# Attention with its exponentials split between ScalarE and VectorE: the planner's costs set anew, DMAs planned by a clock, five buffers for VectorE's weights

## The chip, the cores and the metric

The kernel runs on one core of one Trainium2 chip. The metric is the device time of one execution in microseconds (us), lower is better.

## The reference

Multi-query attention: 8 batches, 1024 positions, 16 heads of 64, all heads of a batch share one key and one value matrix.

```python
q = q.transpose(0, 2, 1, 3)                       # (8, 16, 1024, 64)
scores = np.matmul(q, k.transpose(0, 1, 3, 2)) / np.sqrt(head_dim)
weights = np.exp(scores - np.max(scores, axis=-1, keepdims=True))
weights = weights / np.sum(weights, axis=-1, keepdims=True)
attn_out = np.matmul(weights, v)
```

## The kernel before, in words

**Work.** Two heads make a pair: 64 pairs, 8 of each batch. A pair has 8 key tiles of 128 positions, and each key tile two halves of 512 queries. The unit of work is a score tile, 128 keys by 2 heads by 512 queries in fp32: 64 x 8 x 2 = 1024 of them. TensorE makes one with two matmuls of 64 rows (`score`, L554 to L563) in one of three PSUM slots. Then its exponential is taken, in one of two ways. ScalarE does it in one instruction (`exp_act`, L577) and writes fp16 weights to one of 20 `wt` buffers (`ABUFS`). VectorE does it in groups of two key tiles, four score tiles, called duos in the code: four instructions turn scores into the bits of a first approximation (`fixed`, L586, the planner's "z"), and a polynomial over the mantissas corrects it (`poly`, L599 to L623): f, m, their product (L615), and two halves of l (L617). A linear term is done by GpSimd in four pieces (`linear`, L630). The correction is added to the weights by an accumulating DMA, one for each half (`add`, L642); in the first group and those of the last two pairs VectorE adds it itself (L621). The weights lie in `wd` buffers (`DBUFS`, 4).

**Value products.** `value` (L647) multiplies the weights by the values, which carry a column of ones, so that the row sums come out too. 16 blocks of 128 queries make a pair; 7 blocks (`NG`) share an accumulator, and there are two accumulators. When a group of blocks is complete, VectorE takes reciprocals (L675) and normalises into `osb` (L685), and SP writes a finished pair to memory (L702). `osb` holds three pairs.

**Inputs.** Queries come in groups of 4 pairs: GpSimd loads four parts of a group, converting to fp16 (`load_part`, L488, four buffers), and SP turns each part by a DMA transpose into `qt` (`trans_q`, L497, three buffers). Keys of the next batch are loaded, copied and turned likewise (L429, L443, L451).

**Order.** Every engine's program order is written by a planner that runs before the kernel is built. `plan` (L70) simulates TensorE, ScalarE, VectorE and GpSimd with costs given as constants at the head of the file: `ACT_P` is the spacing of exponentials, `ACT_L` the time from a start to the free slot, `QK_P` a score, `AV_B` one block of a value product, `SWITCH` a change between the two, `PE_L` from a score's start to its reader's, `STEPS` and `VEC` VectorE's instructions. At each step TensorE takes a score for ScalarE, a score for VectorE or a value product; `LAG` is how many pairs the products stay behind the exponentials, `LEAD` how far VectorE's groups may run ahead of ScalarE's pair. A score for VectorE is planned when VectorE is due (`Z_PE`) and ScalarE has work ahead (`Z_ACT`). Additions, loads and transposes aren't part of this simulation: `with_dmas` (L331) puts them into the finished list, additions as soon as GpSimd has room, transposes when the exponentials have come so far as `transfers` (L317) says, in pairs. The list is then issued in order (L727), and each engine and queue executes its part in that order, with semaphores for the data. Within this list the planner's own times play no part any more.

Of the kernel before, what the change touches and what calls it, by code (L numbers as in the profile page):

```python
# [10 lines left out]
FP16 = mybir.dt.float16  # L11
# [6 lines left out]
P = 128  # L18
# [6 lines left out]
VEC = dict(z=1.13, rec=0.12, norm=0.55)  # L25
STEPS = (1.13, 1.13, 1.13, 2.2, 1.13, 1.13, 1.13, 1.13)
VEC_L = 0.19
VEC_DEP = 0.12
ADD_L = 12.0
POOL_S, POOL_F, POOL_L, POOL_D = 0.15, 1.05, 0.12, 1.0  # L30
# [3 lines left out]
ABUFS, DBUFS = 20, 4  # L34
LAG, END = 1.0, 6.0
LEAD, LEAD_0, LEAD_END = 2.5, 1.5, 10.0
FIRST_Q = 6.0
# [3 lines left out]
REM = (4, 3, 2, 2)  # L41
Z_GAP, Z_PE, Z_ACT = 2, 2.0, 1.3
ACC_L = 0.25
FAR = 1e9
# [24 lines left out]

def plan(NP, NKT, stats=None):  # L70
# [13 lines left out]

    pe = act = 0.0
# [11 lines left out]
    gap = 99  # L97
# [12 lines left out]
    pool = lock = 0.0  # L110
# [3 lines left out]
    while todo_g or groups:  # L114
        if pe <= dve:
            T = pe
            prog = ap + (na / nap if ap >= 0 else 0)
            if not vunits and not over:
                lead = min(LEAD if prog > 4 else LEAD_0, LEAD * (NP - prog) / LEAD_END) if duos else 0
                pd = max(dlast + 1, math.ceil(ap + lead))  # L120
                okay = pd < NP and (len(duos) < DBUFS or all(used[t] == NB for t in duos[-DBUFS]))
                if pd // 4 == 0:
                    okay = okay and T >= FIRST_Q * pd
                else:
                    okay = okay and prog >= 4 * (pd // 4) - QLEAD and T >= FIRST_Q * min(pd, 6)
                if pd <= ap:
                    okay = okay and pd == ap and len(ajs) >= 2 and ap < NP - 1
                if okay and prog < NP - STOP:
                    js = [ajs.pop(-2), ajs.pop(-1)] if pd == ap else [NKT - 2, NKT - 1]
                    if pd == ap:  # L130
                        nap -= 4
                    d = len(duos)
                    duos.append([pd * NKT + j for j in js])
                    mine[pd] = mine.get(pd, []) + js
                    for n, j in enumerate(js):
                        owner[pd * NKT + j] = d
                    vunits = [(d, i) for i in range(4)]
                    dlast = pd
# [14 lines left out]
            free = [s for s in range(3) if slot[s] <= T + (SWITCH if mode != "qk" else 0)]  # L153
            kind = None
            if (free and vunits and gap >= Z_GAP and not zs and dve <= T + PE_L + Z_PE and act > T + Z_ACT
                    and len(steps) <= REM[vunits[0][1]]):
                kind = "z"
            elif free and units:
                kind = "act"
            elif free and vunits and ap == NP - 1 and not ajs and not zs and len(steps) <= REM[vunits[0][1]]:  # L160
                kind = "z"
# [9 lines left out]
            for grp in groups:  # L171
# [16 lines left out]
            av = tav <= T + (SWITCH if mode != "av" else 0) and (  # L188
                nv < NB * NKT * (prog - lag) or over
            )  # L190
            do = None
            if kind and (
                mode == "qk" or len(free) >= 2 or not av
                or act - T - SWITCH - PE_L < AV_B * 6 + MARGIN
            ):
                do = "qk"
            elif mode == "qk" and units and min(slot) - T < WAIT:
                pass
            elif av:
                do = "av"  # L200
                first = min(slot)
                if units and first - T < AV_B * 6 and (
                    act - max(first, T) - SWITCH - PE_L < AV_B * 3 + MARGIN
                ):
                    do = None
            if do == "qk":
                s = min(free, key=lambda s: slot[s])
                st = max(T + (SWITCH if mode != "qk" else 0), slot[s])
                pe, mode = st + QK_P, "qk"
                if kind == "z":  # L210
                    d, i = vunits.pop(0)
                    slot[s] = FAR
                    zs.append((st + PE_L, s, (d, i)))
                    gap = 0
                    emit(st, "qk", duos[d][i // 2], i % 2, s)
                else:
                    u = units.pop(0)
                    na += 1
                    act = max(act, st + PE_L)
                    emit(act, "act", *u)  # L220
                    slot[s] = ready[u] = act + ACT_L
                    act += ACT_P
                    gap += 1
                    emit(st, "qk", *u, s)
            elif do == "av":
                st = max(T + (SWITCH if mode != "av" else 0), tav)
# [4 lines left out]
                pe = st + AV_B * nb + (AV_1 if mode == "qk" else 0)  # L231
# [5 lines left out]
                if not left:  # L237
                    acc[a] = FAR
                    r = pe - AV_B + PE_L
# [5 lines left out]
        else:  # L245
            T = dve
            z = [x for x in zs if x[0] <= T]
# [36 lines left out]
            elif what == "step":  # L284
# [8 lines left out]
                if n in (0, 1):  # L293
                    ready[duos[x[0]][n]] = dve + VEC_L + ADD_L * (not late)
# [5 lines left out]
            else:  # L300
                nxt = [x[0] for x in zs + evs if x[0] > T] + [pe + 1e-6] * (pe > T)
                nxt += [x for x in (*avail.values(), pool) if T < x < FAR]
                dve = max(min(nxt, default=0.0), T + 1e-3)
                last = None
        if max(pe, dve) > 900:
            raise RuntimeError((pe, dve, ap, len(duos), steps, halves, vunits, groups, slot))
    for _, k, segs, a, kind in evs:
# [5 lines left out]
    units = [2 * (NKT - len(mine.get(p, []))) for p in range(NP)]  # L313
    return with_dmas(ops, duos, units, direct, NP, NKT), duos


def transfers(NP):  # L317
    QP, HP = 4, 8
    res = []
    for g in range(1, NP // QP):  # L320
        for i in range(QP):
            at = QP * (g - 2) + i + 0.2 if g > 1 else 0.15 + 0.5 * i
            res += [(at, "loadq", g, i), (at + 0.75, "turnq", g, i)]
    for b in range(1, NP // HP):
        at = HP * (b - 1)
        res += [(at + 1.5, "loadk", b), (at + 2.2, "copyk", b), (at + 2.5, "turnk", b, 0),
                (at + 3.5, "turnk", b, 1), (at + 2.9, "loadv", b)]
    return sorted(res)


def with_dmas(ops, duos, units, direct, NP, NKT):  # L331
    fs = [t for t, _, op in ops if op[0] == "l"] + [FAR]
    todo = transfers(NP)
    cost = dict(loadq=0.85, loadk=0.85, copyk=0.95, loadv=1.2)
    res, adds, loads, turns, gone = [], [], [], [], set()
    n, pool, done = 0, 0.0, {}
    last = ops[-1][0]
    for t, _, op in ops + [(last + 20.0 * i, 0, ("end",)) for i in range(1, 4)]:
        if op[0] != "end":
            res.append(op)  # L340
        if op[0] == "l":
            n += 1
            pool = max(pool, t + POOL_S) + POOL_F
        if op[0] == "step" and op[2] in (4, 5) and op[1] not in direct:
            adds.append((t + STEPS[op[2]], op[1], op[2] - 4))
        if op[0] == "act":
            p = op[1] // NKT
            done[p] = done.get(p, 0) + 1
            prog = p + done[p] / units[p]
            while todo and todo[0][0] <= prog:  # L350
                x = todo.pop(0)
                (turns if x[1][:4] == "turn" else loads).append(x[1:])
        while True:
            at = max(pool, t)
            room = fs[n] - at if n < len(fs) else FAR
            if adds and adds[0][0] <= t + 0.3 and room > POOL_D:
                _, d, h = adds.pop(0)
                res.append(("add", d, h))
                pool = at + POOL_D
            elif not adds and loads and room > cost[loads[0][0]] + 0.1:  # L360
                x = loads.pop(0)
                res.append(x)
                gone.add(x)
                pool = at + cost[x[0]]
            else:
                break
        for x in list(turns):
            if ("load" if x[0] == "turnq" else "copy") + x[0][4:] in {y[0] for y in gone if y[1:] == x[1:len(y)]}:
                res.append(x)
                turns.remove(x)  # L370
    assert not (adds or loads or turns or todo), (adds, loads, turns, todo)
    return res
# [3 lines left out]
def kernel(  # L376
# [43 lines left out]
    behind: dict = {}  # L420
    acc: dict = {}
    rec: dict = {}
    left = [NB] * NP

# [20 lines left out]
    def trans_k(b, x):  # L445
# [48 lines left out]
    def trans_q(g, i):  # L494
        if g and i == 0:
            place_q(g)
        nc.sync.dma_start_transpose(  # L497
            out=of_pair(qt[g], i), in_=qn[g, i].rearrange("p c x -> p (c x)")
        )

# [9 lines left out]
    def load_first():  # L510
# [12 lines left out]
        st["k16"] = consts.tile([P, NKT, 2, D], FP16, name="k160")  # L523
# [53 lines left out]
    def exp_act(t, c):  # L577
        nc.scalar.activation(  # L578
            out=wt[t][:, :, c * QC : (c + 1) * QC], in_=sc.pop((t, c)), func=EXP, scale=ascale
        )  # L580
# [59 lines left out]
    def add(d, h):  # L640
        x = slice(h * 2 * S, (h + 1) * 2 * S)
        nc.gpsimd.dma_start(  # L642
            out=flat(wd[d].bitcast(I16))[:, x], in_=tmp[d, "l"].bitcast(I16)[:, x],
            accum_op=ALU.add,
        )
# [58 lines left out]
    ops, duos = plan(NP, NKT)  # L704
    groups = grouped(NP)
# [91 lines left out]
```

## Time and profile before

| | us |
|---|---|
| median of 3 runs (lowest, highest) | 771.21 (769.87, 773.09) |
| the profiled execution | 771.49 |
| its span, first to last instruction | 769.6 |
| ScalarE busy | 751.5 |
| VectorE busy | 713.8 |
| TensorE busy (matmul) | 677.7 |
| GpSimd busy | 380.0 |

The profile is of one execution. "Busy" is the union of an engine's instructions; matmuls are pipelined, so TensorE's figure is not that of a full array. L578 is line 578 of the kernel before. A row of the groups gives line, engine, operation, output<-input, shapes and count, then busy time, the mean of one in ns, and the idle time of the engine just before such instructions with what ended it. A wait row gives who waited, for whom, then the total in us, how often, and the longest. A timeline row gives the start, the time to the end of the merged instructions, engine, line, operation and count, and in brackets the idle time before.

### The profile page before, as it was taken

Reading aid. Unit: us, or ns where it says so; the run is one execution under the profiler, and the core shown is the slowest. Engines: PE = TensorE matmul, PEld = TensorE weight load, DVE = VectorE, ACT = ScalarE, POOL = GpSimd, SP = SyncE. Lnnn points to the kernel's source line nnn. Section 1 sums busy time; section 2 is a strip of 40 time slices with the busy share of each in tenths; the row PEclk is TensorE's granted clock in tenths of the full one; section 3 lists DMA queues with packets and bytes.
Section 4 is the critical chain, followed back from the end, with each engine's and each line's share of the span. In section 5 each row is a group of like instructions: output and inputs, shape, how many; then the busy total and the mean of one; then the engine's idle time right before and its main releaser. Section 6 shows DMA issues by size and latency. Waiting matters only on the chain.

```text
span 769.6 us, 23528 instructions
## 1 busy us (share of the span) xinstructions
PE 677.7 (88%) x10256; PEld 414.3 (54%) x10256; DVE 713.8 (93%) x797; ACT 751.5 (98%) x819; POOL 380.0 (49%) x393
## 2 busy tenths in 40 slices
PE   6869989889989999989999899899898899989987
PEld 2435555555555555555555555555555555555555
DVE  5969999998999999998998999999999999999997
ACT  7969999999999999999999999999999999999996
POOL 3144545655447545556446546465454555453400
PEclk9979999999999999999999999999999999999999
DMA  9878899999999999999898999999989999866443
GB/s 168 120 133 155 150 186 163 169 175 174 162 162 170 191 180 152 193 145 203 144 180 150 190 185 156 170 188 169 182 144 175 186 178 167 163 131 134 112 102 93
DMA packets 185046, 124.07 MB, mean 161 GB/s; under 512 B 89328, under 2 KB 172400, under 8 KB 184944
## 3 DMA queue, kind: packets, MB, share of 16 engines
q0 software_dynamic: 42880, 69.87, 56.7%
q1 hardware_dynamic: 140480, 51.92, 35.5%
q8 instruction: 80, 1.31, 0.7%
q10 hardware_dynamic: 1584, 0.79, 0.4%
q14 instruction: 22, 0.18, 0.1%
HBM read 37.75 MB, written 33.55 MB: 93 GB/s over the span
## 4 chain that ended last, share of the span: by engine, by line
ACT 76%; issue 12%; PE 6%; DMA 1%; DVE 0%; SPq 0%; ACTq 0%
ACT wt L578 76%; PE sc L558 3%; PE acc L666 3%; DMA qt<-qn 1%; DVE osb L685 0%; SPq L702 0%; DVE rec L675 0%; ACTq L578 0%; SPq L497 0%
## 5 line engine op out<-in xcount | busy, mean ns | idle before, releaser
L578 ACT ACTIVATE wt<-sc 128x1024 f16<-128x1024 f32 x816 | 749.0, 1266 | 8.3 <-PE sc L558 8.3
L558 PE MATMUL sc<-qt,k2t 64*128 64x512 f16 x2048 | 372.0, 385 | 82.1 <-ACT wt L578 57.8
L630 POOL TENSOR_SCALAR l<-f 128x1024 f16<-128x1024 uint16 x196 | 212.4, 1083 | 293.0 <-DVE m L615 134.2
L666 PE MATMUL acc<-v,wt 128*128 128x65 f16 x6528 | 307.7, 195 | 0.9 <-issue 0.7
L666 PEld LDWEIGHTS <-wt 128*128 128x128 f16 x6528 | 236.8, 98 | 129.0 <-issue 128.5
L586 DVE TENSOR_SCALAR wd<-sc 128x1024 uint16<-128x1024 f32 x208 | 253.6, 1219 | 31.3 <-PE sc L558 30.3
L558 PEld LDWEIGHTS <-k2t 64*128 64x128 f16 x2048 | 129.1, 93 | 183.4 <-issue 136.6
L617 DVE TENSOR_TENSOR l<-m,l 128x2048 int16<-128x2048 f16 x104 | 126.0, 1213 | 7.6 <-POOL l L630 7.1
L615 DVE TENSOR_TENSOR m<-f,m 128x4096 f16<-128x4096 uint16 x52 | 118.7, 2283 | 0.2
L642 POOL DMA_DIRECT2D wd<-l x98 | 94.5, 964 | 39.2 <-DVE l L617 24.9
L666 PE MATMUL acc<-v,wd 128*128 128x65 f16 x1664 | 100.1, 194 | 0.0
L685 DVE TENSOR_TENSOR osb<-acc,rec 128x448 f32<-128x448 f32 (+4 forms) x165 | 91.6, 566 | 2.6
L666 PEld LDWEIGHTS <-wd 128*128 128x128 f16 x1664 | 69.4, 97 | 32.8 <-issue 32.8
L488 POOL DMA_DIRECT2D qn<-in_q_dram x60 | 59.9, 1000 | 18.7 <-DMA qt<-qn 9.5
L604 DVE TENSOR_SCALAR f<-wd 128x4096 uint16<-128x4096 uint16 x52 | 64.0, 1231 | 0.3
L607 DVE TENSOR_SCALAR m<-f 128x4096 f16<-128x4096 uint16 x52 | 64.0, 1230 | 0.3
L675 DVE RECIPROCAL rec<-acc 128x7 f32<-128x7 f32 (+1 forms) x147 | 28.4, 195 | 3.7 <-PE acc L666 3.5
L437 POOL DMA_DIRECT2D v<-in_v_dram x8 | 9.3, 1163 | 0.0
L621 DVE TENSOR_TENSOR wd<-wd,l 128x2048 uint16<-128x2048 uint16 x6 | 7.2, 1210 | 0.0
L429 POOL DMA_DIRECT2D k<-in_k_dram x7 | 5.7, 821 | 0.1
L544 PE MATMUL kps<-ident,k 128*128 128x128 f16 x8 | 1.2, 308 | 4.1 <-DVE k L532 4.1
L443 POOL COPY k<-k 128x64 f16<-128x64 f16 x7 | 4.2, 599 | 1.2 <-DMA k<-in_k_dram 1.0
(19 smaller groups left out, 17.8 us busy)
## 6 DMA issues: line engine op xcount, KB each, us to landing
wd<-l POOLq DMA_DIRECT2D x98, 512.0 KB, 6.6
out_dram<-osb SPq DMA_DIRECT2D x63, 512.0 KB, 6.4
qn<-in_q_dram POOLq DMA_DIRECT2D x63, 256.0 KB, 7.3
v<-in_v_dram POOLq DMA_DIRECT2D x8, 128.0 KB, 6.6
qt<-qn SPq DMA_TRANSPOSE x63, 5.2
k<-in_k_dram POOLq DMA_DIRECT2D x7, 128.0 KB, 8.7
osb<-in_q_dram ACTq DMA_DIRECT2D x2, 256.0 KB, 4.0
osb<-in_k_dram SPq DMA_DIRECT2D x2, 128.0 KB, 3.1
```

Source lines behind the costliest of these rows:

```text
L488: nc.gpsimd.dma_start(out=qn[g, i], in_=q[b, :, 2 * QP * r : 2 * QP * (r + 1), :].rearrange("(c p) h d -> p c (h d)", p=P)[:, n * i : n * ...
L558: nc.tensor.matmul(sc[t, c][:, h, :].rearrange("p (i x) -> p i x", x=P), keys(p // HP, h, j), queries(p, c)[64 * h : 64 * h + 64, :, :], s ...
L578: nc.scalar.activation(out=wt[t][:, :, c * QC : (c + 1) * QC], in_=sc.pop((t, c)), func=EXP, scale=ascale)
L586: behind["dve"] = nc.vector.tensor_scalar(out=wt[t].bitcast(U16)[:, :, c * QC : (c + 1) * QC], in0=sc.pop((t, c)), scalar1=vscale, scalar2 ...
L604: i = V.tensor_scalar(out=new(d, "f", U16, 1), in0=z, scalar1=1023, scalar2=None, op0=ALU.bitwise_and)
L607: i = V.tensor_scalar(out=new(d, "m", FP16, 1), in0=tmp[d, "f"], scalar1=-ONE, scalar2=1.0 / ONE, op0=ALU.add, op1=ALU.mult)
L615: i = V.tensor_tensor(out=tmp[d, "m"], in0=tmp[d, "f"], in1=tmp[d, "m"], op=ALU.mult)
L617: i = V.tensor_tensor(out=tmp[d, "l"].bitcast(I16)[:, h], in0=tmp[d, "m"][:, h], in1=tmp[d, "l"][:, h], op=ALU.mult)
L630: n = nc.gpsimd.tensor_scalar(out=tmp[d, "l"][:, x], in0=tmp[d, "f"][:, x], scalar1=GB / ONE, scalar2=GA, op0=ALU.mult, op1=ALU.add,)
L642: nc.gpsimd.dma_start(out=flat(wd[d].bitcast(I16))[:, x], in_=tmp[d, "l"].bitcast(I16)[:, x], accum_op=ALU.add,)
L666: nc.tensor.matmul(acc[k][:, n + x - lo, 0 : D + 1], w[:, h, i * P : (i + 1) * P], kst[p // HP]["v"][:, j, 0 : D + 1], start=first and x = ...
L685: behind["dve"] = nc.vector.tensor_tensor(out=osb[:, x % (OSB * NB) : x % (OSB * NB) + m, :], in0=a[:, n : n + m, 0:D], in1=r[:, n : n + m ...
```

## The change

The constants are replaced: spacing of exponentials 0.915 to 0.905, the latencies split by who reads, `DBUFS` 4 to 5, `LAG` 1.0 to 1.7, and others. The planner's choice at TensorE compares when ScalarE would run dry for either order, and a slot that becomes free while TensorE waits costs a `WAKE`. `with_dmas` is gone: additions, loads and transposes are issued inside the simulation by `issue`, with a clock for SP (`sp`), for the DMA engines busy with additions (`busy`) and for those busy with a transpose (`hold`). In the kernel a transpose gets two dependencies more, on the last addition issued and on an exponential two back in the list, and an addition that was held back by a transpose gets one on such an exponential. The first batch's doubled keys (`k160`) lie in the part of `osb` that pair 2 uses later.

By the order of instructions that comes out, the changed kernel has 54 groups on VectorE (52 before), 216 score tiles there (208), 808 exponentials on ScalarE (816), and 102 accumulating DMAs (98). The value products, loads and transposes are the same in number.

```diff
-ACT_P, ACT_L = 0.915, 1.15
-QK_P, AV_B, AV_1, SWITCH, PE_L = 0.23, 0.035, 0.02, 0.10, 0.51
-MARGIN, WAIT = 0.35, 0.3
+ACT_P, ACT_L, ACT_R = 0.905, 1.07, 1.15
+QK_P, AV_B, SWITCH, PE_L, PE_Z, PE_R = 0.215, 0.03, 0.11, 0.49, 0.44, 0.24
+MARGIN, WAIT, WAKE = 0.3, 0.5, 0.27
...
-ADD_L = 12.0
+POOL_D = dict(add=1.0, loadq=0.85, loadk=0.85, copyk=0.95, loadv=1.2)
+ADD_0, ADD_1, ADD_L = 2.7, 2.2, 6.0
+TURN_0, TURN_1, TURN_L, LOAD_L = 1.0, 4.0, 8.0, 8.0
...
-ABUFS, DBUFS = 20, 4
-LAG, END = 1.0, 6.0
-LEAD, LEAD_0, LEAD_END = 2.5, 1.5, 10.0
-FIRST_Q = 6.0
+ABUFS, DBUFS = 20, 5
+LAG, END = 1.7, 8.0
+LEAD, LEAD_0, LEAD_END = 3.0, 1.5, 10.0
+FIRST_Q, FIRST_G = 3.5, 22.0
...
-Z_GAP, Z_PE, Z_ACT = 2, 2.0, 1.3
-ACC_L = 0.25
+Z_GAP, Z_PE, Z_ACT = 2, 2.0, 1.0
+ACC_L = 0.15
...
-            at = QP * (g - 2) + i + 0.2 if g > 1 else 0.15 + 0.5 * i
-            res += [(at, "loadq", g, i), (at + 0.75, "turnq", g, i)]
+            at = QP * (g - 2) + 0.85 * i - 0.6 if g > 2 else 1.2 + 0.7 * i if g > 1 else 0.02 + 0.01 * i
+            res += [(at, "loadq", g, i), (at + (0.7 if g > 1 else 0.0), "turnq", g, i)]
...
+    def issue(t):
+        nonlocal pool, sp, busy, hold
+        while todo_d and todo_d[0][0] <= prog:
+            x = todo_d.pop(0)[1:]
+            (turns if x[0][:4] == "turn" else loads).append(x)
+        if turns and t >= max(sp, busy - TURN_0):
+            x = turns[0]
+            at = landed.get(x[1:3] if x[0] == "turnq" else ("copyk", x[1]), FAR)
+            if at <= t:
+                turns.pop(0)
+                emit(t, *x)
+                if x[0] == "turnq":
+                    freed.append(t + TURN_L)
+                sp = t + TURN_0
+                hold = t + TURN_1
+        if pool > t or halves and zs:
+            return
+        if adds and adds[0][0] <= t and t >= hold - ADD_0:
+            at, d, h = adds.pop(0)
+            emit(t, "add", d, h, at < hold - ADD_0)
+            pool = t + POOL_D["add"]
+            busy = max(busy, t + ADD_0) + ADD_1
+            ready[duos[d][h]] = busy + ADD_L
+        elif loads and not adds and can(loads[0], t):
...
-            if kind and (
-                mode == "qk" or len(free) >= 2 or not av
-                or act - T - SWITCH - PE_L < AV_B * 6 + MARGIN
-            ):
+            if kind == "z":
                 do = "qk"
-            elif mode == "qk" and units and min(slot) - T < WAIT:
-                pass
+            elif kind == "act":
+                s = min(range(3), key=lambda s: slot[s])
+                at = aq if slot[s] <= aq else slot[s] + WAKE
+                if av:
+                    then = after if slot[s] <= after else slot[s] + WAKE
+                if slot[s] <= aq:
+                    do = "qk" if mode == "qk" or len(free) >= 2 or not av or then + PE_L > act - MARGIN else "av"
+                elif av and (then <= at + 0.02 or then + PE_L <= act):
+                    do = "av"
+                elif slot[s] - T < WAIT:
+                    do = "qk"
             elif av:
                 do = "av"
...
-def with_dmas(ops, duos, units, direct, NP, NKT):
...
+    def after(i, xs):
+        for x in xs:
+            tc.add_manual_dep(
+                i.ins, x.ins.name,
+                mybir.DependencyInfo(mybir.DependencyClass.Sync, mybir.DependencyReason.DATA),
+                reason="transposes and additions apart",
+            )
...
-        nc.sync.dma_start_transpose(
+        i = nc.sync.dma_start_transpose(
             out=of_pair(qt[g], i), in_=qn[g, i].rearrange("p c x -> p (c x)")
         )
+        after(i, past[-2:-1] + added[-1:])
...
-        st["k16"] = consts.tile([P, NKT, 2, D], FP16, name="k160")
+        st["k16"] = osb[:, 2 * NB : 2 * NB + NKT, :].bitcast(FP16).rearrange("p c (r d) -> p c r d", r=2)
...
-    def add(d, h):
+    def add(d, h, held):
         x = slice(h * 2 * S, (h + 1) * 2 * S)
-        nc.gpsimd.dma_start(
+        added.append(nc.gpsimd.dma_start(
             out=flat(wd[d].bitcast(I16))[:, x], in_=tmp[d, "l"].bitcast(I16)[:, x],
             accum_op=ALU.add,
-        )
+        ))
+        if held:
+            after(added[-1], past[-2:-1])
```

More of the change, by code (lines that the diff above doesn't have):

```diff
@@ L109, in plan @@
     direct: set = set()
-    pool = lock = 0.0
+    pool = lock = sp = busy = hold = prog = 0.0
+    todo_d = transfers(NP)
+    freed = [0.0] * 4
+    adds: list = []
+    loads: list = []
+    turns: list = []
+    landed: dict = {}
     dlast = -1
@@ L225, in plan @@
             elif do == "av":
-                st = max(T + (SWITCH if mode != "av" else 0), tav)
+                st = aa
                 grp, n, j = pick
@@ L293, in plan @@
                 if n in (0, 1):
-                    ready[duos[x[0]][n]] = dve + VEC_L + ADD_L * (not late)
+                    if late:
+                        ready[duos[x[0]][n]] = dve + VEC_L
+                    else:
+                        adds.append((dve + VEC_L, x[0], n))
                 last = x
@@ L331, in with_dmas @@
-def with_dmas(ops, duos, units, direct, NP, NKT):
[L332 to L372, printed above, removed]
@@ L375 @@
+    return ops, duos
 @with_exitstack
@@ L420 @@
     behind: dict = {}
+    past: list = []
+    added: list = []
     acc: dict = {}
```

98 lines of the change are left out of this document (55 added, 43 removed).

## The prediction

> **What bounds the kernel now.** I read the page first (busy shares and costliest groups), then the waits of every engine, then ScalarE's timeline.
>
> ```profile
> span 769.6 us, 23528 instructions
> PE 677.7 (88%) x10256; PEld 414.3 (54%) x10256; DVE 713.8 (93%) x797; ACT 751.5 (98%) x819; POOL 380.0 (49%) x393
> ACT 76%; issue 12%; PE 6%; DMA 1%; DVE 0%; SPq 0%; ACTq 0%
> L578 ACT ACTIVATE wt<-sc 128x1024 f16<-128x1024 f32 x816 | 749.0, 1266 | 8.3 <-PE sc L558 8.3
> ```
>
> ScalarE (ACT) is busy 98% of the span, nearly all of it with the 816 exponentials of L578, and it holds 76% of the chain that ended last. VectorE (DVE) stands at 93%. So the time is the number of ScalarE's exponentials by their spacing, plus ScalarE's gaps, plus head and tail. The timeline gives the spacing:
>
> ```profile
> 103.49 660.14 ACT L578 ACTIVATE wt<-sc 128x1024 f16<-128x1024 f32 x720 [0.28 <-PE sc L558]
> ```
>
> From 103.49 on, 720 exponentials run without a break that this view separates. They overlap, so I divide: 660.14 / 720 = 0.917 us each, small stalls included. The next view, waits by engine, shows where ScalarE and TensorE (PE) stood still:
>
> ```profile
> PE sc L558 <- ACT wt L578: 57.8, 234, 0.7
> ACT wt L578 <- PE sc L558: 8.3, 6, 5.9
> PE sc L558 <- DMA qt<-qn: 6.4, 1, 6.4
> PEld L666 <- DMA wd<-l: 0.2, 1, 0.2
> ```
>
> ScalarE lost 8.3 us in 6 waits for scores, 5.9 of it at once; TensorE waited once, 6.4 us, for a transpose. The timeline shows that these are one event:
>
> ```profile
> 38.98 0.41 SPq L702 DMA_DIRECT2D out_dram<-osb  x1
> 39.48 3.70 SPq L497 DMA_TRANSPOSE qt<-qn  x1
> 45.63 1.04 PE L558 MATMUL sc<-qt,k2t 64*128 64x512 f16 x4 [6.41 <-DMA qt<-qn]
> 46.71 4.15 ACT L578 ACTIVATE wt<-sc 128x1024 f16<-128x1024 f32 x4 [5.92 <-PE sc L558]
> 51.36 2.86 ACT L578 ACTIVATE wt<-sc 128x1024 f16<-128x1024 f32 x3 [0.51 <-PE sc L558]
> ```
>
> In SP's program order the fourth transpose of query group 1 stands behind the output DMA of pair 0, and that DMA waits for VectorE's normalisation. The transpose is issued at 39.48, the score that reads it starts at 45.63, ScalarE sits idle 5.92 us and then 0.51 more.
>
> **The change, part by part.** All sums are against the profiled execution: 771.49 us with a span of 769.6, so 1.9 us lie outside the span. The median of the runs shown is 771.21, 0.3 lower.
>
> *Fewer exponentials on ScalarE.* In the new order there are 54 groups of VectorE's weights instead of 52 (four score tiles each): 216 tiles on VectorE instead of 208, 808 on ScalarE instead of 816. 8 x 0.917 = **-7.3 us**, all on the path.
>
> *The head stall.* In the new SP order the four transposes of group 1 are rows 5 to 8, ahead of the first output DMA (row 12), and their last one stands behind ScalarE's 15th exponential, 16 before the first score that reads the group; before it stood behind the 35th. 16 x 0.917 = 14.7 us of lead, against a landing time of
>
> ```profile
> DMA to landing us min/median/max: 3.0/5.2/13.6
> ```
>
> for the transposes of qt (min, median, max). So the two gaps go: 5.92 + 0.51 = 6.4 us. The four exponentials after the stall took 4.15 us, about 1.04 apart, in place of 0.917: four times 0.12 is another 0.5. Together **-6.9 us**. What is late next at that place is nothing the order shows: group 2 has its last transpose 20 exponentials before its first use, in both kernels.
>
> Now 769.6 - 7.3 - 6.9 = **755.4** if nothing else moves. Three things could add to it.
>
> *VectorE's share.* The two added groups cost VectorE, by the page's groups:
>
> ```profile
> L586 DVE TENSOR_SCALAR wd<-sc 128x1024 uint16<-128x1024 f32 x208 | 253.6, 1219 | 31.3 <-PE sc L558 30.3
> L617 DVE TENSOR_TENSOR l<-m,l 128x2048 int16<-128x2048 f16 x104 | 126.0, 1213 | 7.6 <-POOL l L630 7.1
> L615 DVE TENSOR_TENSOR m<-f,m 128x4096 f16<-128x4096 uint16 x52 | 118.7, 2283 | 0.2
> L604 DVE TENSOR_SCALAR f<-wd 128x4096 uint16<-128x4096 uint16 x52 | 64.0, 1231 | 0.3
> L607 DVE TENSOR_SCALAR m<-f 128x4096 f16<-128x4096 uint16 x52 | 64.0, 1230 | 0.3
> ```
>
> A group is 4 x 1.219 + 1.231 + 1.230 + 2.283 + 2 x 1.213 = 12.05 us. How full VectorE is in the steady stretch, and what it waits for between 100 and 700 us:
>
> ```profile
> 150.00:750.00 600.00, 539.93 (x8263) 332.46 (x8261) 571.13 (x637) 600.00 (x656) 310.80 (x313) 1.00 0.95 165
> DVE wd L586 <- PE sc L558: 17.1, 32, 1.4
> DVE l L617 <- POOL l L630: 6.8, 10, 1.2
> DVE rec L675 <- PE acc L666: 2.1, 3, 1.1
> ```
>
> (The first row's columns are PE, PEld, DVE, ACT, POOL busy, then granted clock, DMA share, GB/s.) That is 571.13 / 656 = 0.871 us of VectorE per exponential. Two more groups over fewer exponentials add 12.05 x (54/808 - 52/816) = 0.037. The new order takes something back: a normalisation stood directly behind its own reciprocal 75 times, and does so 49 times now. What that costs:
>
> ```profile
> 759.37 0.20 DVE L675 RECIPROCAL rec<-acc 128x7 f32<-128x7 f32 x1
> 759.48 1.18 DVE L621 TENSOR_TENSOR wd<-wd,l 128x2048 uint16<-128x2048 uint16 x1
> 762.89 0.20 DVE L675 RECIPROCAL rec<-acc 128x6 f32<-128x6 f32 x1 [0.57 <-PE acc L666]
> 763.12 0.56 DVE L685 TENSOR_TENSOR osb<-acc,rec 128x384 f32<-128x384 f32 x1
> ```
>
> 0.23 us to a dependent instruction, 0.11 to an independent one: 26 x 0.12 = 3.1 us, 0.004 per exponential. VectorE's work is then 0.904 per exponential against ScalarE's 0.917: it fits, with 0.013 to spare. Its waits must fit too. Those for GpSimd (POOL) and for the accumulators, 8.9 us in 600 or 0.014 each, don't depend on VectorE being early; with them it needs 0.918, 0.001 too much, over some 770 exponentials about 0.8 us. Those for scores (17.1 us, 0.026 each) are mostly the sign of an engine with time to spare; if they all stayed, VectorE would pace the kernel at 0.944, 0.027 x 770 = 21 us. Bounds 0 and 21; I take **+2.2**, near the lower row, because the score that VectorE reads is ordered by when VectorE is due.
>
> *TensorE.* It changes between scores and value products 1457 times instead of 1231: 113 more round trips.
>
> ```profile
> 93.72 0.39 PE L558 MATMUL sc<-qt,k2t 64*128 64x512 f16 x2
> 94.05 0.60 PE L666 MATMUL acc<-v,wt 128*128 128x65 f16 x14
> 94.64 0.61 PE L558 MATMUL sc<-qt,k2t 64*128 64x512 f16 x4
> 95.18 0.51 PE L666 MATMUL acc<-v,wd 128*128 128x65 f16 x11
> ```
>
> One score and the change to products take 0.33 us, two take 0.54, so a score is 0.21 and a change 0.12; with as much for the way back, 113 x 0.24 = 27 us. The cover is TensorE's own waiting for ScalarE, 57.8 us in 234 waits: 0 on the path. Without that cover each microsecond would be ScalarE's.
>
> *The later start of the value products.* They lag 1.7 pairs: the first one stands behind the 22nd exponential instead of the 11th, and until then TensorE has only scores. Its clock (third column from the right) can halve in such a stretch:
>
> ```profile
> 13.90:17.30 3.40, 2.25 (x14) 0.57 (x11) 2.88 (x3) 3.40 (x5) 1.93 (x3) 1.00 0.79 121
> 95.80:99.20 3.40, 1.92 (x17) 0.76 (x16) 3.40 (x7) 3.40 (x5) 2.00 (x2) 1.00 1.03 194
> 99.20:102.70 3.50, 3.48 (x41) 2.11 (x41) 3.46 (x3) 3.25 (x4) 0.00 (x0) 0.51 1.00 214
> ```
>
> A stretch with 2.25 of 3.4 us busy kept it, one with 1.92 lost it right after. At half clock an exponential came 0.12 late (above): over 11 of them 1.3 us, nothing if the clock stays. I take **+0.5**. The Trainium skill ("TensorE: Matmul & The Clock Gate", What's actually happening) says that the clock is halved after an idle window of about 3.4 us; by it a stage of scores alone, without such an idle stretch, costs nothing, and the sum would be 0.5 lower. The trace agrees for the 6.41 us gap and not at 99.20, where no idle window preceded.
>
> *At nothing.* Four more additions: between an addition and the first product that reads it lie at least 12 exponentials in either order, 11 us, against
>
> ```profile
> wd<-l POOLq DMA_DIRECT2D x98, 512.0 KB, 6.6
> ```
>
> 6.6 us to landing; TensorE lost 0.2 us to them. If that cover went, a late addition would cost what it is late. The fifth buffer only lets the planner start a group earlier. The separation of transposes from additions: only one wait for a transpose exists, and it comes from SP's order, so faster transposes save 0; what the new waits may cost is a rival. The first keys' move into the output buffer, tile read long before pair 2 writes there: 0.
>
> Sum: 755.4 + 2.2 + 0.5 = 758.1 span, + 1.9 = **760.0 us**.
>
> **The rivals.** (a) *VectorE paces.* If half of its waits for scores stay, 0.013 x 770 = 10 us: 755.4 + 0.8 + 10 + 0.5 + 1.9 = 769. For: work at 98.6% of ScalarE's spacing; against: the waits were idle time of an engine with reserve. (b) *The stall moves instead of going*: transposes of group 1 still late, 760.0 + 6.9 = 767. For: GpSimd's loads of that group wait for the transposes of group 0. Against: 14.7 us of lead. (c) *Slower: the new waits on SP.* Each transpose now waits for the last addition to land (6.6 us) and for an exponential, in one queue with the output DMAs; behind it wait later transposes and outputs. A group that comes late costs what the head stall cost, 6.9 us. A group's last transpose stands 16 to 39 exponentials ahead of the first score that reads it, so three queued landings would have to add up at one place; from three such groups on of the fifteen the gain of 11 is more than gone: 760.0 + 21 = 781. That transposes beside other DMAs need no care is what the Trainium skill says ("DMA: Bandwidth & Descriptors", Rules for kernel authors); by it the waits are pure risk. No row here prices them.
>
> **How the numbers follow.** Chances: forecast, 755 to 764, 0.67; (a) 0.16; (b) 0.05; (c) 0.06; VectorE keeping all its waits, 755.4 + 21 + 0.5 + 1.9 = 779, 0.03; below 755 0.03. Low end: small stalls in the 0.917 gone and the two additions 0, 755; high end: (a) with its clock term at 1.3, 770.5. About 0.5% is what a measurement of this kernel tells from no change, 767.4 to 775.1. Faster: 0.67 + 0.03 + a good half of (a) and of (b), 0.81; same, the rest of these, 0.10; slower 0.06 + 0.03 = 0.09.
>
> **What would show it.** Right: 808 exponentials at 0.915 to 0.92; no gap of several us before 100 us; VectorE 97 to 98% busy from 150 to 700 with its waits for scores well under 17.1 us. (a): ScalarE idle for scores many times, scores waiting for VectorE's buffers (1.5 us before). (b), (c): TensorE waiting for qt. Wrong altogether: TensorE waiting for additions, or GpSimd held long enough that VectorE waits for its halves.

## The result

The changed kernel takes 758.32 us (median of 6 runs, 757.86 to 759.06) against 771.07 for the kernel before in the same comparison: ratio 0.9832, 95% interval 0.9816 to 0.9849, so 1.7% faster. The profiled execution took 759.06 with a span of 757.2; forecast for it were 760.0 and 758.1. A few single executions of the kernels below lie well above the others of the same kernel and count as slow: the ratios leave them out, the medians do not, and where a reading depends on them they are listed.

The page of the changed kernel, its span, busy shares and two of its groups (VectorE's first step L586 is now L608, ScalarE's exponential L578 is L600):

```profile
span 757.2 us, 23618 instructions
PE 682.4 (90%) x10256; PEld 417.7 (55%) x10256; DVE 728.2 (96%) x815; ACT 744.0 (98%) x811; POOL 401.7 (53%) x405
L600 ACT ACTIVATE wt<-sc 128x1024 f16<-128x1024 f32 x808 | 741.5, 1237 | 2.7 <-PE sc L580 2.7
L608 DVE TENSOR_SCALAR wd<-sc 128x1024 uint16<-128x1024 f32 x216 | 262.8, 1217 | 12.8 <-PE sc L580 11.7
```

ScalarE is still the engine that is never idle; it waits 2.7 us for scores in the whole span, 8.3 before. Its timeline, from where the head is over:

```profile
102.53 547.56 ACT L600 ACTIVATE wt<-sc 128x1024 f16<-128x1024 f32 x597
650.39 100.02 ACT L600 ACTIVATE wt<-sc 128x1024 f16<-128x1024 f32 x109 [0.30 <-PE sc L580]
```

547.56 / 597 is 0.917 us for each exponential, the spacing of before. This row also splits the 12.4 us between the spans. At 102.53 the changed kernel has 808 - 597 - 109 = 102 exponentials behind it; at 103.49 the kernel before had 816 - 720 = 96. So the head is shorter by 0.96 + 6 x 0.917 = 6.5 us. Eight exponentials fewer are 7.3. The last exponential ends at 750.41, 6.8 before the end, where it was 6.0: the tail is 0.8 longer. The gap of 0.30 at 650 and a slightly wider spacing take back some 0.6. Together 12.4.

What VectorE waits for between 100 and 700 us in the changed kernel, and its busy time from 150 to 750 (third figure):

```profile
DVE wd L608 <- PE sc L580: 3.9, 13, 0.8
DVE rec L699 <- PE acc L690: 0.7, 2, 0.5
```

```profile
150.00:750.00 600.00, 550.58 (x8527) 343.33 (x8526) 591.83 (x661) 599.70 (x655) 325.46 (x319) 1.00 0.95 169
```

Before, these waits were 17.1 + 6.8 + 2.1 = 26.0 us; now they are 4.6, and VectorE is busy 591.8 of 600 us, 98.6%. The forecast's 0.904 / 0.917 was 98.6% too.

The head of the changed kernel on its timeline, the first product and then the stretch from 31 to 36 us:

```profile
27.55 0.56 PE L690 MATMUL acc<-v,wt 128*128 128x65 f16 x7
...
30.94 0.95 PE L690 MATMUL acc<-v,wt 128*128 128x65 f16 x14
31.05 1.22 DVE L608 TENSOR_SCALAR wd<-sc 128x1024 uint16<-128x1024 f32 x1 [1.13 <-PE sc L580]
31.82 0.61 PE L580 MATMUL sc<-qt,k2t 64*128 64x512 f16 x2
32.37 0.56 PE L690 MATMUL acc<-v,wt 128*128 128x65 f16 x7
32.47 2.06 ACT L600 ACTIVATE wt<-sc 128x1024 f16<-128x1024 f32 x2 [0.83 <-PE sc L580]
...
35.78 0.39 PE L690 MATMUL acc<-v,wt 128*128 128x65 f16 x7
36.10 0.39 PE L580 MATMUL sc<-qt,k2t 64*128 64x512 f16 x2
```

Until 34 us a score takes 0.61 and seven products 0.56; from then on both take 0.39. So TensorE ran at its slow clock until the products had kept it busy for a while, and ScalarE lost 0.83 us at once there and some more around it. This trace holds no record of the clock before 34.5 us, and a window there shows 1.00 in its place; the lengths tell more. The trace of b1 (below; up to there the same order) has the record, and the same lengths (the first figure after the window's length is TensorE's busy time, the third from the right the clock):

```profile
19.95:23.37 3.42, 2.19 (x10) 0.33 (x8) 3.38 (x3) 3.42 (x5) 0.00 (x0) 0.50 1.33 168
26.78:30.19 3.41, 2.96 (x22) 1.37 (x23) 1.45 (x2) 3.41 (x5) 0.02 (x1) 0.50 1.34 167
30.19:33.61 3.42, 3.42 (x31) 1.44 (x27) 1.23 (x1) 2.57 (x4) 0.21 (x1) 0.50 1.22 143
33.61:37.02 3.41, 3.41 (x56) 2.04 (x55) 3.12 (x4) 3.41 (x4) 0.00 (x0) 1.00 0.44 85
```

### The profile page after: what moved, and what is told of

The parts are those of the page before. It is cut to its first block, busy times and chain, and to the rows that moved or that the text cites. A ratio compares the mean times of both kernels' runs of the same rounds, so it can differ in the third digit from the quotient of the medians.

```text
span 757.2 us, 23618 instructions
## 1 busy us (share of the span) xinstructions
PE 682.4 (90%) x10256; PEld 417.7 (55%) x10256; DVE 728.2 (96%) x815; ACT 744.0 (98%) x811; POOL 401.7 (53%) x405
## 4 chain that ended last, share of the span: by engine, by line
ACT 81%; PE 10%; issue 7%; DVE 0%; DMA 0%
ACT wt L600 81%; PE sc L580 5%; PE acc L690 5%; DMA osb<-in_q_dram 0%; DVE osb L709 0%; DVE wd L608 0%; ACT qn L556 0%; PE qps L570 0%; ACT qt L572 0%; PE kps L566 0%; DVE rec L699 0%; DVE k2t L568 0%
## 5 line engine op out<-in xcount | busy, mean ns | idle before, releaser
L600 ACT ACTIVATE wt<-sc 128x1024 f16<-128x1024 f32 x808 | 741.5, 1237 | 2.7 <-PE sc L580 2.7
L580 PE MATMUL sc<-qt,k2t 64*128 64x512 f16 x2048 | 375.4, 389 | 63.5 <-ACT wt L600 52.5
L690 PE MATMUL acc<-v,wt 128*128 128x65 f16 x6464 | 318.0, 195 | 0.6 <-issue 0.6
L608 DVE TENSOR_SCALAR wd<-sc 128x1024 uint16<-128x1024 f32 x216 | 262.8, 1217 | 12.8 <-PE sc L580 11.7
L664 POOL DMA_DIRECT2D wd<-l x102 | 111.7, 1126 | 71.2 <-DVE l L639 24.1
L639 DVE TENSOR_TENSOR l<-m,l 128x2048 int16<-128x2048 f16 x108 | 128.8, 1194 | 1.0 <-POOL l L652 0.9
L637 DVE TENSOR_TENSOR m<-f,m 128x4096 f16<-128x4096 uint16 x54 | 124.0, 2297 | 0.0
L690 PE MATMUL acc<-v,wd 128*128 128x65 f16 x1728 | 103.5, 194 | 0.0
L629 DVE TENSOR_SCALAR m<-f 128x4096 f16<-128x4096 uint16 x54 | 67.6, 1252 | 0.2
L509 POOL DMA_DIRECT2D qn<-in_q_dram x60 | 55.7, 929 | 18.4 <-DMA qt<-qn 15.5
```

What stands on the lines that cost most here:

```text
L509: nc.gpsimd.dma_start(out=qn[g, i], in_=q[b, :, 2 * QP * r : 2 * QP * (r + 1), :].rearrange("(c p) h d -> p c (h d)", p=P)[:, n * i : n * ...
L580: nc.tensor.matmul(sc[t, c][:, h, :].rearrange("p (i x) -> p i x", x=P), keys(p // HP, h, j), queries(p, c)[64 * h : 64 * h + 64, :, :], s ...
L600: past.append(nc.scalar.activation(out=wt[t][:, :, c * QC : (c + 1) * QC], in_=sc.pop((t, c)), func=EXP, scale=ascale))
L608: behind["dve"] = nc.vector.tensor_scalar(out=wt[t].bitcast(U16)[:, :, c * QC : (c + 1) * QC], in0=sc.pop((t, c)), scalar1=vscale, scalar2 ...
L629: i = V.tensor_scalar(out=new(d, "m", FP16, 1), in0=tmp[d, "f"], scalar1=-ONE, scalar2=1.0 / ONE, op0=ALU.add, op1=ALU.mult)
L637: i = V.tensor_tensor(out=tmp[d, "m"], in0=tmp[d, "f"], in1=tmp[d, "m"], op=ALU.mult)
```

## Experiments

The theory at the start: the gain is eight exponentials and the head stall, the added waits do nothing. Rivals: the separation of transposes and additions gives part of it; the new costs and the finer order do. All times are medians, each beside the kernel before on the same chip (771.3 to 771.6).

**The head alone** (a2): the kernel before, with `transfers` changed.

```diff
-            at = QP * (g - 2) + i + 0.2 if g > 1 else 0.15 + 0.5 * i
-            res += [(at, "loadq", g, i), (at + 0.75, "turnq", g, i)]
+            at = QP * (g - 2) + i + 0.2 if g > 2 else 1.2 + 0.7 * i if g > 1 else 0.02 + 0.01 * i
+            res += [(at, "loadq", g, i), (at + (0.75 if g > 1 else 0.0), "turnq", g, i)]
```

> The kernel before, with only the due times of query groups 1 and 2 changed to those of the changed kernel; 816 exponentials as before. Theory: the stall of 5.92 + 0.51 us and the slow clock after it go, 771.1 - 6.9 = 764.2. Rival (the stall only moves to the next late transpose, since SP's queue is the cause): 768 to 771, with TensorE waiting for qt at another place.

Measured 764.97 against 771.63, ratio 0.9908 (0.9879 to 0.9938): 6.7 us. ScalarE's waits for scores in this kernel's groups:

```profile
L578 ACT ACTIVATE wt<-sc 128x1024 f16<-128x1024 f32 x816 | 749.0, 1267 | 3.1 <-PE sc L558 3.0
```

8.3 us of waits are 3.1. TensorE waits for no transpose of queries there any more: the stall went and did not move.

**Four buffers** (a6): the changed kernel, replanned.

```diff
-ABUFS, DBUFS = 20, 5
+ABUFS, DBUFS = 20, 4
```

> The changed kernel with four buffers for VectorE's weights instead of five. The planner then finds room for 51 groups, 820 exponentials on ScalarE, 12 more. Theory (the time is the number of exponentials): 758.3 + 12 x 0.917 = 769.3. Rival (the gain comes from the new costs and the finer order, not from the number): 758 to 763.

Measured 768.68 against 771.63, ratio 0.9958 (0.9940 to 0.9976). Against 758.32 that is 10.4 us for 12 exponentials, 0.86 each. The whole order is planned anew here, so more than the count differs, but the count accounts for the time. Without the fifth buffer the new planner puts more exponentials on ScalarE than the old one did.

**Five buffers in the old plan** (d1): a2 and two more edits.

```diff
-ABUFS, DBUFS = 20, 4
+ABUFS, DBUFS = 20, 5
...
-        st["k16"] = consts.tile([P, NKT, 2, D], FP16, name="k160")
+        st["k16"] = osb[:, 2 * NB : 2 * NB + NKT, :].bitcast(FP16).rearrange("p c (r d) -> p c r d", r=2)
```

> The kernel before with three edits: the due times of query groups 1 and 2, five buffers for VectorE's weights, and the first keys in the output buffer to make room; costs, lag and choice at TensorE as before, no added waits. 53 groups, 812 exponentials, 4 fewer. Theory (the fifth buffer gives room by itself, each exponential 0.917): 765.0 - 3.7 = 761.3. Rival (with the old costs VectorE keeps its waits for scores and can't take the added group): 765 or more.

Measured 764.53 against 771.3, ratio 0.9914 (0.9895 to 0.9933): 0.4 below a2, not 3.7, and by the ratios (0.9914 and 0.9908) no gain at all. ScalarE waits longer for scores than in a2, 5.8 us against 3.0, which is most of the missing 3.3. TensorE's timeline, in the profiled execution of 767.55, shows one of the places:

```profile
572.33 0.42 PE L666 MATMUL acc<-v,wt 128*128 128x65 f16 x8
574.12 0.30 PE L666 MATMUL acc<-v,wd 128*128 128x65 f16 x4 [1.36 <-DMA wd<-l]
574.25 0.50 PE L666 MATMUL acc<-v,wt 128*128 128x65 f16 x11
574.68 0.60 PE L558 MATMUL sc<-qt,k2t 64*128 64x512 f16 x4
```

A product waited 1.36 us for an addition, and the next scores stood behind it. The fifth buffer is needed, but it does not give the gain alone. The rival had the time, but not the reason: VectorE kept its waits, 16.9 us for scores between 100 and 700 us (17.5 in a2), and took the added group all the same; what shows is a late addition. All of VectorE's waits between 100 and 700 us, for scores, GpSimd and accumulators, are 26.0 us before, 23.6 here, 36.5 with the new planner and four buffers (a6), and 4.6 only where the fifth buffer and the new planner come together. Which of the planner's parts does it, no run isolates.

**Products one pair behind** (a5): the changed kernel.

```diff
-LAG, END = 1.7, 8.0
+LAG, END = 1.0, 8.0
```

> The changed kernel with value products 1.0 pair behind throughout (the first one behind the 11th exponential); 54 groups, 808 exponentials as before. Theory (the later products give nothing: the number of exponentials and the head stall are the gain): 758 within 1 us. Rival (the lag of 1.7 pairs is the slack that VectorE's weights need to arrive in): 762 or more, with TensorE waiting for additions.

Measured 764.39 (six executions, 761.11 to 772.42), ratio 0.9903 (0.9876 to 0.9930): 6 us of the gain gone with the same 808 exponentials. The rival was right that the lag matters. The profile is of the slowest of the six, 772.42. The windows of five places where ScalarE lost time (PE, PEld, DVE, ACT, POOL busy, granted clock, DMA share, GB/s):

```profile
86.00:98.00 12.00, 9.19 (x114) 5.30 (x116) 9.59 (x12) 9.90 (x12) 3.70 (x4) 0.72 1.16 206
186.00:193.00 7.00, 5.82 (x62) 2.76 (x62) 6.60 (x8) 6.61 (x8) 2.76 (x4) 0.76 1.09 198
268.00:275.00 7.00, 6.33 (x74) 3.42 (x73) 5.93 (x8) 6.44 (x8) 2.84 (x3) 0.76 1.06 201
525.00:532.00 7.00, 6.72 (x86) 4.00 (x86) 5.98 (x6) 5.75 (x8) 2.59 (x3) 0.76 1.07 125
640.00:660.00 20.00, 13.81 (x201) 8.38 (x198) 13.51 (x16) 13.32 (x15) 6.72 (x6) 0.83 1.18 182
```

At each of them TensorE's clock was halved for part of the stretch, and ScalarE was busy 67 to 94% of it. But the two longest losses begin with a late DMA. In the last stretch VectorE waited for an output DMA, and in the first TensorE waited for an addition, which is the rival's reason, shown once:

```profile
ACT wt L600 <- PE sc L580: 13.2, 15, 5.6
DVE osb L709 <- DMA out_dram<-osb: 6.5, 1, 6.5
PE acc L690 <- DMA wd<-l: 2.2, 1, 2.2
```

Of ScalarE's 13.2 us, 6.6 lie in the last stretch and 2.1 in the first. In the three between, TensorE's gaps are at most 0.53 us and its clock halves all the same. The changed kernel has neither of the two DMA waits, and its clock is 1.00 from 100 to 750 us. Two stretches of a5 just before a halving, with no late DMA near, and the stretch of the changed kernel in which TensorE had the least to do (its busy time is the first figure after the length):

```profile
184.70:188.11 3.41, 1.86 (x19) 0.91 (x19) 2.88 (x5) 3.41 (x5) 2.35 (x3) 1.00 1.06 195
266.62:270.03 3.41, 1.85 (x19) 0.88 (x16) 3.32 (x7) 3.41 (x5) 2.32 (x3) 1.00 1.05 155
```

```profile
218.82:222.23 3.41, 2.52 (x27) 1.14 (x24) 3.41 (x6) 3.41 (x5) 1.95 (x2) 1.00 0.98 136
```

The fourteen traces of this case agree. In all of them the clock changes at multiples of 3.41 us. Cut into stretches of that length, there are 39 at full clock that a halving follows (the one at each kernel's end left out), and TensorE was busy 2.33 us or less in each; of the 2935 that keep the full clock all but 34 lie above 2.33 (these 34 lie from 1.82 up, so the two kinds overlap). At half clock the full clock came back after stretches with 3.06 us or more, and not after 3.05 or less. Products 1.7 pairs behind give TensorE a stock of work that needs no recent data, and no stretch of the changed kernel from 34.5 to 754 us falls below 2.5. That this is why its clock stays up fits all of these numbers; no run varied TensorE's busy time alone.

**Early products only in the head** (a4): the changed kernel, meant to win back the slow clock at 14 to 34 us.

```diff
-            lag = min(LAG, LAG * (NP - prog) / END)
+            lag = min(LAG, LAG * (NP - prog) / END, 1.0 if prog < 3 else 1.0 + 0.2 * (prog - 3))
```

> The changed kernel with value products only 1.0 pair behind during the first three pairs, growing to 1.7 afterwards; the first product stands behind the 11th exponential instead of the 22nd; 808 exponentials. Theory (TensorE's clock stays halved until the products begin, and that costs 1.7 us of ScalarE at 29 to 34 us): the clock is full by about 17 us and the time 756.6. Rival (those gaps come from something else in the head, such as the wait for VectorE's slot): 758.3.

Measured 758.99 (one of the six at 774.05), ratio 0.9830 (0.9797 to 0.9863): no gain. The products did bring the clock up earlier, though not by 17 us: they begin at 17.76, and the first single score of 0.39 is this one, instead of that at 36.10 in the changed kernel:

```profile
23.49 0.39 PE L580 MATMUL sc<-qt,k2t 64*128 64x512 f16 x2
```

But the clock halves again four times between 36 and 524 us, and the edit is worth nothing.

**A slower ScalarE in the plan** (d3): the changed kernel with `ACT_P` 0.914 and `LAG` 1.0, a try for a better version.

```diff
-ACT_P, ACT_L, ACT_R = 0.905, 1.07, 1.15
+ACT_P, ACT_L, ACT_R = 0.914, 1.07, 1.15
...
-LAG, END = 1.7, 8.0
+LAG, END = 1.0, 8.0
```

> The changed kernel with ACT_P 0.914, nearer to the 0.917 that the trace shows, and value products 1.0 pair behind; 808 exponentials. Theory (the small stalls of ScalarE that are left, some 2 us in the head and 0.7 at 650 us, come from an order made for a faster ScalarE): 756 to 757.5. Rival (what is left doesn't hang on that cost): 758 to 759.

Measured 764.64, ratio 0.9894 (0.9863 to 0.9925): as a5, so nothing can be said on `ACT_P`; the lag hides it. The ten executions go from 757.68 and 757.85, as fast as the changed kernel, over 760.77 to 770.21: an order with the short lag can reach that time, but seldom does. No kernel here beats the changed one.

**Without the added waits** (a1): the changed kernel, same order.

```diff
     def after(i, xs):
-        for x in xs:
+        for x in []:
```

> The changed kernel, its order untouched, without the added waits that hold transposes and additions apart. Theory (the gain is eight fewer exponentials on ScalarE and the head stall): the added waits are off ScalarE's path, so the same within 0.5 us of the changed kernel's 758.3. Rival (the separation gives part of the gain, by faster transposes and additions): slower by 2 us or more, with TensorE or GpSimd waiting for transposes or additions.

Measured 789.41, and the six executions are 768.55, 780.49, 788.46, 790.37, 795.83 and 808.18. The theory failed here: even the fastest is 9.5 us above the slowest of the changed kernel (759.06), and five of the six are slower than the kernel before. The profile is of the execution of 780.49, where ScalarE waits 22.3 us for scores (2.7 in the changed kernel); of the fastest there is none, so what costs its 10 us is not seen. From 530 us of the profiled one, with the 20 us from 550 by themselves, then the changed kernel at about the same stage of its work:

```profile
530.00:580.00 50.00, 35.60 (x494) 20.73 (x491) 34.35 (x38) 37.77 (x42) 18.32 (x18) 0.85 1.27 138
550.00:570.00 20.00, 17.33 (x274) 10.80 (x270) 16.04 (x18) 19.68 (x23) 10.54 (x10) 1.00 1.23 100
```

```profile
510.00:560.00 50.00, 45.38 (x677) 27.94 (x676) 49.11 (x56) 50.00 (x56) 28.72 (x28) 1.00 0.94 172
```

The DMA share is 1.27 against 0.94 and the bytes moved are fewer, 138 GB/s against 172: the DMA engines are busier and get less done. From 550 to 570 this is so with ScalarE still busy 19.68 of 20 us, so it is not a mere result of the engines' standing still. From the timeline of a1, what follows for the engines:

```profile
577.90 0.22 DVE L709 TENSOR_TENSOR osb<-acc,rec 128x64 f32<-128x64 f32 x1 [11.02 <-DMA out_dram<-osb]
578.17 0.55 PE L690 MATMUL acc<-v,wt 128*128 128x65 f16 x7 [9.36 <-DVE osb L709]
579.73 2.12 ACT L600 ACTIVATE wt<-sc 128x1024 f16<-128x1024 f32 x2 [9.06 <-PE sc L580]
```

VectorE waits 11 us for an output DMA to free its buffer, TensorE for VectorE's accumulator, ScalarE for scores. The landing of the transposes of qt (min, median, max) in a1, then in the changed kernel:

```profile
DMA to landing us min/median/max: 3.1/8.3/27.0
```

```profile
DMA to landing us min/median/max: 3.0/4.7/13.4
```

**Which wait does it** (b1, b2). In b1 a transpose waits for the last addition only, in b2 for the exponential only (each is changed at the transposes of queries and of keys; one place is shown):

```diff
-        after(i, past[-2:-1] + added[-1:])
+        after(i, added[-1:])
...
-        if held:
-            after(added[-1], past[-2:-1])
```

```diff
-        after(i, past[-2:-1] + added[-1:])
+        after(i, past[-2:-1])
```

> The changed kernel, order untouched, of whose added waits only one kind is left: a transpose waits for the last addition to land. No wait on an exponential, for transposes or for held additions. Theory (what keeps the DMAs from piling up is that a transpose starts when the addition ahead of it has landed): 758 to 760. Rival (it is the pace that the exponentials set for SP and GpSimd): 768 or more, as without any of the waits.

> The opposite half: transposes wait for an exponential two back in the list, held additions too, but no transpose waits for an addition to land. Theory (the landing is what counts): 765 or more, with landings of transposes well above the 4.7 us of the changed kernel. Rival (the pace counts): 758 to 760.

Measured b1 758.16 (757.56, 757.65, 758.07, 758.24, 758.49, 773.17), b2 758.26 (757.68, 757.69, 758.26, 758.35, 808.43); ratios 0.9829 (0.9815 to 0.9843) and 0.9827 (0.9813 to 0.9842). Either kind is enough for the usual time, so neither theory holds as stated: b2 should have been slow. Nor is it the landing as such: in b2 the transposes of qt land in 6.2 us in the median, in the changed kernel in 4.7, at the same time. One execution of each stands far above. The changed kernel had none such in six, but a4, with both waits, had one (774.05), so these runs can't say whether both waits together make them rarer.

**The waits in the old order** (b3): a2 with both waits at each transpose.

```diff
...
+        after(i, past[-2:-1] + added[-1:])
...
```

> The kernel before with the due times of query groups 1 and 2 and, at each transpose, the changed kernel's two waits (the last addition landed, an exponential two back). 816 exponentials. Theory (in this order the transposes fall between the additions anyway, so the waits neither give nor cost): 765.0 within 1 us. Rival (the waits themselves give time by faster transposes): 763 or less; or they cost: 767 or more, with TensorE waiting for qt.

Measured 765.56, ratio 0.9935 (0.9908 to 0.9963); a2 is 764.97. As expected, nothing given, though the transposes land sooner, in 4.1 us in the median against 5.3 in a2. Five of the eight executions lie between 764.0 and 765.7; the others are 770.66, 771.66 and 777.64, where a2 had none above 766.18 in six, so a small cost is not ruled out.

**How much VectorE can bear** (a7 the changed kernel, a8 the kernel before): every reciprocal issued twice.

```diff
+        nc.vector.reciprocal(out=rec[k][:, 0:n], in_=acc[k][:, 0:n, D])
         behind["dve"] = nc.vector.reciprocal(out=rec[k][:, 0:n], in_=acc[k][:, 0:n, D])
```

> The changed kernel with every reciprocal of VectorE issued twice in a row: 147 instructions more, 0.11 us each, 16.5 us of VectorE's time; nothing is left out. Theory (VectorE has only the reserve that its idle time shows, some 1.2% of 600 us, 7 us, and paces the kernel beyond it): 758.3 + 16.5 - 7 = 768, between 765 and 775. Rival (VectorE has cover): 758 to 761.

> The kernel before with every reciprocal issued twice: the same 16.5 us more on VectorE. Theory (here VectorE is idle 4.8% of the steady stretch, 29 us in 600, so the load fits): 771 to 773. Rival (VectorE's idle time before is not free, being waits for scores that stay): 771 + 16 = 787.

Measured a7 782.17, 23.9 over the changed kernel; a8 789.94 against 771.5, ratio 1.0263 (1.0224 to 1.0301), 18.4 more. The pages of a7 and a8:

```profile
PE 681.2 (87%) x10256; PEld 406.3 (52%) x10256; DVE 752.7 (96%) x962; ACT 753.6 (97%) x811; POOL 407.8 (52%) x405
```

```profile
PE 671.7 (85%) x10256; PEld 402.6 (51%) x10256; DVE 738.8 (94%) x944; ACT 758.8 (96%) x819; POOL 380.6 (48%) x393
```

VectorE's busy time grew by 752.7 - 728.2 = 24.5 us and 738.8 - 713.8 = 25.0, not the 16.5 that I had put. Of 24.5 the changed kernel hid 0.6; of 25.0 the kernel before hid 6.6, though VectorE idled 29 us in 600 there. (By the spans of the profiled executions alone, 22.9 and 19.6 us longer, they hid 1.6 and 5.4.) Where the delay enters, in the waits of TensorE (a7, then a8):

```profile
PE sc L580 <- DVE wd L608: 49.9, 125, 0.9
```

```profile
PE sc L558 <- DVE wd L586: 61.4, 119, 1.4
```

TensorE waits for a slot that VectorE still holds, 49.9 and 61.4 us instead of 0.9 and 1.5; its waits for ScalarE's slots shrink, from 52.5 to 26.8 and from 57.8 to 21.6. Both theories fell: VectorE has little reserve in either order, a quarter of the load at most, because the next score stands behind its slot in TensorE's program. This load was not replanned for; whether a planner that knew of it could hide more, no run shows.

## Why the prediction was right, point by point

- **The sum:** the span came to 757.2 for 758.1 forecast. Some of this closeness is luck: the term for VectorE was over 1.5 us too high, and the tail, 0.8 us longer, stood in no term. The high end of the range, by its own terms 755.4 + 0.8 + 10 + 1.3 + 1.9, is 769.4 and not 770.5; nothing hangs on it.
- **Eight exponentials, -7.3:** right. The spacing is 0.917 before and 0.918 after, small stalls included, and a6 priced twelve at 10.4.
- **The head stall, -6.9:** right, and caused by SP's order: moving the loads and transposes of groups 1 and 2 alone gave 6.7 (a2). Rival (b), the stall that only moves, fell with it.
- **VectorE, +2.2:** too much; the spacing hardly changed, so the term is about 0.3, or 0.6 with the gap at 650. The work was forecast well (98.6%), and its waits fell from 26.0 to 4.6 us in 600, below even the lower row that I had kept, since waits for GpSimd are gone from the view. Rival (a) did not come about: scores waited 0.9 us for VectorE's buffers, 1.5 before. But the reason I gave for the fit, an idle engine with 0.013 to spare for each exponential, is weak by a7 and a8: in the fixed order idle time was little reserve, and rival (a), in which VectorE paces, is what a7 shows as soon as VectorE is late.
- **The later products, +0.5:** the mechanism, the slow clock, is there, but not as a clock that is lost. In the changed kernel no score before 34 us is short. In b1 the clock was up from 9.7 to 13.1 us only, and then the scores alone kept TensorE busy 2.2 to 2.7 us of each 3.41, too little to bring it back. In the kernel before it was up at 13.9 after the same work; why, these runs don't say. The price was about right: the head came out at 6.5 of 6.9, so 0.4 for the 0.5 of the sum. That the lag is worth 6 us by the median elsewhere (a5) I had not seen at all.
- **TensorE's 113 round trips at nothing:** held; it waits 52.5 us for ScalarE (its scores' row on the page after) against 57.8. The 27 us priced for them do not show either: its busy time grew by 4.7.
- **The fifth buffer at nothing:** wrong as an edit by itself. Without it there are 51 groups and 10.4 us more (a6). The sum was not hurt, since it counted the groups from the finished order.
- **The separation at nothing, its waits a risk (rival c):** the 0 held only with the waits in place, and the rival, in which they cost time, did not come. Beside the kernel before, faster transposes give nothing, as forecast (b3). But the new order needs some wait: without any, 768.6 to 808.2 us (a1). SP does wait, as these rows of its queue show (transposes L518 in the changed kernel). TensorE never waits for a transpose of queries; only GpSimd's loads do, 15.5 us in two waits, off ScalarE's path:

```profile
SPq L518 <- DMA wd<-l: 232.6, 35, 14.1
SPq L518 <- ACT wt L600: 85.7, 60, 5.4
POOL qn L509 <- DMA qt<-qn: 15.5, 2, 8.2
```

- **The rules cited:** the Trainium skill ("DMA: Bandwidth & Descriptors", Rules for kernel authors) says that a transpose next to ordinary DMAs needs nothing. It says so beside a rule on transposes that corrupt each other; by time, the measurement decides against it here, 768.6 us at best without the waits (a1) against 759.1 at worst in the changed kernel. The Trainium skill ("TensorE: Matmul & The Clock Gate", What's actually happening) says that the slow clock is the default and that it comes back after an idle window of about 3.4 us. The scores of 0.61 us before 34 us agree with the first; the halvings of a5 near 188 and 270 us do not agree with the second, since they follow stretches whose longest gap is 0.53 us and in which TensorE was busy 1.86 and 1.85 of 3.41.

## What to carry to other kernels

Where one engine is busy 98%, count its instructions in the finished order and multiply by their measured spacing; a long gap in its timeline is worth following to the queue order that causes it. Idle time of a second engine may be little reserve when another engine's program order waits for its buffers: load it once on purpose and look. Waits that look like pure risk can be what an order's time rests on, so take them out once before calling them free.

## What the runs showed of the hardware that I had not expected

- Transposes and accumulating DMAs that neither wait holds back can get into a stretch where the DMA share rises (1.27) while the bytes fall (138 GB/s against 172) and single transposes take up to 27 us (a1). Overlap as such is not enough: in b2 transposes wait for no addition, and four of five executions are as fast as the changed kernel. What in the DMA engines does this is open.
- TensorE's clock can halve without a long gap, in a5 five times behind the head with no late DMA near. All 39 halvings of the fourteen traces follow a stretch of 3.41 us with 2.33 us or less of TensorE's modelled busy time. From half clock it came back after 3.06 us or more, which scores alone (2.2 to 2.7 us in b1) did not reach. Whether busy time is what the chip counts is open.
